# The output product of a gated decoder block as seven products of halves

## The chip, the cores and the metric

The kernel runs on one core of a Trainium2 chip, in one launch. The metric is the device time of an execution in microseconds; each run reports one, and a kernel is judged by the median of its runs. TensorE is written PE, VectorE DVE, ScalarE ACT, GpSimd POOL; PEld is PE's weight load, and SP is the engine that issues most of the DMAs.

## The reference, cut to what matters

A decoder block of 2048 tokens and 1024 channels, in float32. A combined input projection feeds a convolution branch and a dilated attention branch; both are projected, gated and added to y, and y goes through the output product:

```python
y = jax.nn.sigmoid(m_conv) * y_conv + jax.nn.sigmoid(m_attn) * y_attn   # (1, 2048, 1024)
out = y @ w_out                                                         # w_out: (1024, 1024)
x = (x + gate[:, None] * out).astype(dt)                                # gate: (1, 1024)
```

`gate` has one value per output channel, the same for all tokens. It comes from the conditioning vector and is known early in the kernel.

## The kernel before, in words

Each float32 operand of a large product is split into a high part (a copy rounded to the type that PE takes, fp32r) and a low part (the rest), and a product is the sum of three: high by high, high by low, low by high. A product of depth 1024 is therefore 8 x 3 = 24 matmuls of 128x128 by 128x512 for a tile of 128x512.

The kernel's last three stages are these.

- **ya** (attention projection), then **yc** (convolution projection). yc runs over t, four stretches of 512 tokens, and in each over dm, eight blocks of 128 output channels: 24 matmuls, then two DVE operations (the gate `mc` times the sum, plus the stored `ya`), then a store to `y_d` in DRAM. The tiles `yl` (loads of `ya_d`) and `yc` of a block come from one tag, `yt`, of four buffers. Eight banks of PSUM are handed out under four tags of two each; yc's blocks go round three of them (`z`, `s`, `o`).
- **out** (lines 1396 to 1415): over j, 16 blocks of 128 tokens. y is loaded for two blocks at a time into the buffer `wide`, transposed already (channels on partitions); ACT and DVE split it; for each half of 512 output channels 24 matmuls sum into one bank, DVE multiplies by `gate_row` (L1413), adds the residual x (L1414), and the tile is stored.

The engines other than PE get their order from the framework's planner, which lets an instruction go ahead of others of its engine as soon as its inputs and its buffer are there. PE's order is the program's, up to the end of yc before the change. To place side work between PE's matmuls, the kernel keeps a plan: `at_block(n, m, f)` calls f ahead of matmul m of block n (n = 8 t + dm). So the norm of the convolution branch for stretch t is worked out during t - 1 (`norms[t].load`, `.mean`, `.variance` with an rsqrt on POOL, `.spread` with matmuls that need it, `.apply`), and w_out is split during the last stretch:

`split_big(h, l, src)` (L1102 to L1109) loads a tile of 128x512 into a raw buffer, copies it on ACT (high part) and subtracts on DVE (low part). Its raw buffer has the tag `fraw`; in these stages it comes from the pool `ys`, with three buffers:

```python
            raw = big.get("raw", big["fr"]).tile([P, 512], F32, tag="fraw", name="fraw", bufs=3 if "raw" in big else 2)
```

The places for split weights: `wcp` (four pairs of tiles, used by the first half of w_conv_out until dm = 3 of the last stretch), `quarter_tile(kh, t, ...)` (places of the input projection's operands, (0, 2) free after dm = 3 as well, (0, 0) and (1, 0) used by the second half of w_conv_out to the end of yc), `wop` (opened at the start of the last stretch, after the norm's data `lnp` is closed) and `op` (opened there too, on the memory of the norm's scratch and of u for even stretches).

The input projection, earlier in the kernel, is done already as seven products of halves (`quad`, L954: `paab`, `pbab`, `pcab` and their like), with the sums of the weight made on POOL and products that share a bank added up there. Its constant list `PRODUCTS` names the seven pairs.

## Time and profile before

| what | value |
| --- | --- |
| median of 3 runs | 2435.33 us (2433.37 to 2435.88) |
| span of the profiled execution, from first to last instruction | 2433.6 us |
| PE busy | 2395.2 us (98%), 12881 matmuls |
| PEld busy | 2138.5 us (88%) |
| DVE busy | 1688.0 us (69%) |
| ACT busy | 975.0 us (40%) |
| POOL busy | 766.9 us (32%) |
| mean granted TensorE clock | 0.994 |
| DMA moved | 372.99 MB, 153 GB/s on average |

The profiled execution has its span as its time; the three runs are times of other executions and stand within 2.3 us of it. Matmuls overlap their neighbours, so the busy share of PE is no measure of its peak: the distance from one matmul's start to the next is. In grouped rows the columns are the count, the busy time in us with the mean of one in ns, and the idle time of the engine ahead of them with what ended it. In rows by tile they are minimum, median and maximum in ns, then the first and the last start. In rows by stretch they are the length, the busy time and count of PE, PEld, DVE, ACT and POOL, the granted clock, the DMA engines' busy share and GB/s.

### The profile page before, as it was taken

What the parts mean: (1) busy time and instruction counts of PE and PEld (TensorE: products, weight loads), DVE (VectorE), ACT (ScalarE), POOL (GpSimd) and SP (SyncE); (2) the same over time, 40 slices, a digit from 0 to 9 for tenths busy, and PEclk for the clock granted to TensorE, in tenths of its full rate; (3) what the DMA queues carried; (4) which work ended last, traced back from release to release, by engine and by line L of the source; (5) the groups of instructions that cost most, each with busy time, mean ns of one, the idle gap of its engine ahead of it and who ended that gap; (6) DMA issues with size and microseconds to landing.
All of it is one profiled execution on the core that took longest, in us unless ns stands there. A gap on an engine that the chain in (4) does not pass through costs nothing.

```text
span 2433.6 us, 39444 instructions
## 1 busy us (share of the span) xinstructions
PE 2395.2 (98%) x12881; PEld 2138.5 (88%) x12881; DVE 1688.0 (69%) x3891; ACT 975.0 (40%) x2738; POOL 766.9 (32%) x899
## 2 busy tenths in 40 slices
PE   7999999999999999999999999999999999999999
PEld 3989999999999999999888888878888888888887
DVE  5855655555555565557779999989999968864333
ACT  5733333433344344345544444554444444331000
POOL 4421111111111111112467777765655620000000
PEclk8999999999999999999999999999999999999999
DMA  7633543444452222116663544664444479866443
GB/s 260 219 111 109 160 126 100 147 145 144 147 151 85 68 71 58 32 47 197 200 197 129 161 156 160 208 204 128 141 143 143 152 251 321 274 197 214 126 147 100
DMA packets 342219, 372.99 MB, mean 153 GB/s; under 512 B 29752, under 2 KB 243032, under 8 KB 342014
## 3 DMA queue, kind: packets, MB, share of 16 engines
q1 hardware_dynamic: 328718, 346.80, 45.9%
q10 hardware_dynamic: 13296, 23.66, 2.7%
q8 instruction: 103, 1.69, 0.3%
q14 instruction: 102, 0.84, 0.1%
HBM read 231.74 MB, written 138.61 MB: 152 GB/s over the span
## 4 chain that ended last, share of the span: by engine, by line
PE 92%; DVE 1%; ACT 1%; POOL 1%; DMA 1%; issue 0%; SPq 0%; POOLq 0%; DVEq 0%; ACTq 0%
PE pz L369 31%; PE yc L1230 7%; PE out L1230 7%; PE paab L954 7%; PE ya L1230 4%; PE pag_g_d L954 4%; PE pcab L954 4%; PE pag_mc_d L954 4%; PE pag_ma_d L954 3%; PE ps L441 3%; PE po L460 3%; PE pzg L369 3%; PE pbab L954 2%; PE pcg_mc_d L954 2%; PE pcg_g_d L954 2%; PE ptq L431 2%
## 5 line engine op out<-in xcount | busy, mean ns | idle before, releaser
L369 PE MATMUL pz<-wh_u,hT_lo 128*128 128x384 f32 x1536 | 537.6, 350 | 4.4 <-DVE hT_lo L288 2.5
L369 PE MATMUL pz<-wh_u,hT_hi 128*128 128x384 f32 x1536 | 519.5, 338 | 4.5 <-ACT wh_u L345 2.0
L369 PE MATMUL pz<-wl_u,hT_hi 128*128 128x384 f32 x1536 | 520.5, 339 | 0.4 <-DVE wl_u L348 0.4
L397 DVE SCALAR_TENSOR_TENSOR qk<-pz,st,wqk 128x128 f32<-128x128 f32 x384 | 117.0, 347 | 320.5 <-POOL st L113 320.4
L112 POOL TENSOR_SCALAR st<-st 128x2 f32<-128x2 f32 x192 | 47.7, 248 | 813.9 <-ACT sq L386 813.9
L369 PEld LDWEIGHTS pz<-wh_u,hT_hi 128*128 128x128 f32 x1536 | 291.5, 190 | 7.2 <-ACT wh_u L345 2.9
L369 PEld LDWEIGHTS pz<-wh_u,hT_lo 128*128 128x128 f32 x1536 | 290.0, 189 | 7.4 <-DVE hT_lo L288 3.2
L369 PEld LDWEIGHTS pz<-wl_u,hT_hi 128*128 128x128 f32 x1536 | 290.7, 189 | 1.9 <-DVE wl_u L348 1.4
L433 ACT ACTIVATE qkT<-ptq 128x256 f32<-128x256 f32 x192 | 73.9, 385 | 419.9 <-PE ptq L431 419.4
L1032 DVE SCALAR_TENSOR_TENSOR ce<-us,pair_taps,ce 128x512 f32<-128x512 f32 x240 | 180.3, 751 | 1.7
L1003 DVE SCALAR_TENSOR_TENSOR ce<-ut,chan,ce 128x512 f32<-128x512 f32 x240 | 180.1, 751 | 0.0
L1016 DVE SCALAR_TENSOR_TENSOR cq<-ut,chan,cq 128x512 f32<-128x512 f32 x208 | 156.6, 753 | 4.2
L918 POOL TENSOR_TENSOR slT<-wT,shT 128x512 fp32r<-128x512 f32 x97 | 128.7, 1328 | 75.7 <-ACT shT L917 74.6
L386 ACT ACTIVATE sq<-pz 128x128 bf16<-128x128 f32 x384 | 106.2, 276 | 100.3 <-PE pz L369 93.4
L113 POOL TENSOR_TENSOR st<-st,mhalf 128x2 f32<-128x2 f32 x192 | 136.5, 711 | 16.0
L917 ACT ACTIVATE shB<-wB 128x512 fp32r<-128x512 f32 x120 | 75.5, 630 | 150.4 <-issue 44.5
L917 ACT ACTIVATE shT<-wT 128x512 fp32r<-128x512 f32 x100 | 63.1, 631 | 153.1 <-issue 64.6
L918 POOL TENSOR_TENSOR slB<-wB,shB 128x512 fp32r<-128x512 f32 x77 | 102.0, 1324 | 68.0 <-ACT shB L917 66.4
L446 ACT ACTIVATE sm<-sm,osb 128x128 f32<-128x128 f32 (+1 forms) x192 | 88.8, 463 | 62.6 <-DVE osb L444 59.5
L1413 DVE TENSOR_TENSOR ot<-out,gate_row 128x512 f32<-128x512 f32 x32 | 22.1, 692 | 116.2 <-PE out L1230 116.2
L460 PE MATMUL po<-lv,pT 128*128 128x128 f32 x600 | 97.2, 273 | 0.0
L460 PEld LDWEIGHTS po<-lv,pT 128*128 128x128 f32 x600 | 93.0, 189 | 0.5 <-issue 0.5
(624 smaller groups left out, 6288.7 us busy)
## 6 DMA issues: line engine op xcount, KB each, us to landing
wB<-in_w_in_dram SPq DMA_DIRECT2D x140, 256.0 KB, 3.8
qkv_d<-qkv SPq DMA_DIRECT2D x128, 192.0 KB, 2.2
wT<-tT_d SPq DMA_DIRECT2D x80, 256.0 KB, 2.8
raw_u<-in_w_in_dram SPq DMA_DIRECT2D x93, 192.0 KB, 3.3
lqk<-qkv_d SPq DMA_DIRECT2D x128, 128.0 KB, 2.3
tT_d<-wB ACTq DMA_DIRECT2D x60, 256.0 KB, 2.3
acc_d<-osb SPq DMA_DIRECT2D x192, 65.0 KB, 1.6
at<-acc_d SPq DMA_DIRECT2D x64, 195.0 KB, 3.5
```

The source lines that it names most:

```text
L113: nc.gpsimd.tensor_tensor(dst, scratch[:, :n], mhalf[:, :n], op=ALU.pow)
L369: nc.tensor.matmul(pz[:, :width], part(a, k, P * j, P), w[:, :width], start=(m == 0), stop=(m == 23))
L386: nc.scalar.activation(sq, pz[:, P * i : P * i + P], AF.Square, scale=1.0 / math.sqrt(P), accum_out=st[:, i : i + 1])
L397: nc.vector.scalar_tensor_tensor(qk[:, 2 * i : 2 * i + 2].rearrange("p a b -> p (a b)"), pz[:, P * i : P * i + P], st[:, 2 + i : 3 + i], w ...
L460: nc.tensor.matmul(po[:, :P], box["pT"][:, P * i : P * i + P], vt, start=(i == 0), stop=(i == nk - 1))
L917: nc.scalar.activation(h, q[name], AF.Copy)
L918: eng.tensor_tensor(l, q[name], h.bitcast(F32), op=ALU.subtract)
L954: nc.tensor.matmul(ps, w, x, start=(m == 0 and ps.name not in first), stop=(m == 11 and not more), skip_group_check=True)
L1003: stt(box["e"], e[:, 1 + j : 513 + j], chan[:, cb, 2 * j : 2 * j + 1], box["e"], op0=ALU.mult, op1=ALU.add)
L1016: stt(box["o"], o[:, 2 + j : 514 + j], w, psum_o, op0=ALU.mult, op1=ALU.add)
L1032: stt(dst, box["both"][:, 1 + j : 513 + j], pair_taps[:, cb, j : j + 1], box["e"], op0=ALU.mult, op1=ALU.subtract if j == 0 else ALU.add)
L1230: nc.tensor.matmul(pz, w, xx, start=(m == 0), stop=(m == len(terms) - 1))
```

## The change: what it does

The output product is computed by the Winograd form of Strassen's scheme, seven products of halves for eight. Tokens are halved (block j and block j + 8), inner channels are halved (k = 0 to 3 and 4 to 7), and so are output channels. For each of eight pairs of token blocks ("quads") there are seven products of 12 matmuls, 128x128 by 128x512, each into one of three banks; products that belong to the same output tile are added up in the bank, and DVE adds the bank to the residual x in SBUF after each product.

- The sums of y (S1 to S4) are made on POOL, four operations of 128x512 per quad; `y_split(j, n)` then splits the operand of product n on ACT and DVE, five products ahead (`LEAD`).
- The weight is multiplied by `gate` and its sums (T1 to T4) are made during yc. `gate_rows` loads the gate twice 128x512; `wo_fetch(k)` loads 1 MB of w_out into the buffer `wide`; `wo_sums(k)` runs six POOL operations on it, with T3, T2 and T4 in buffers of the tag `fraw` of `ys`, and stores all seven 128x512 tiles to `wo_d` in DRAM. There are four k, fetched at blocks 11, 14, 17, 20 and summed at 12, 15, 18, 21.
- `wo_split(name, k)` splits a tile of `wo_d` with `split_big`: 20 during the last stretch of yc (B11, B21, T2, then T1 and T3), eight during the first quad (B22, T4), whose places yc holds to its end.
- y is loaded by `y_load(j)` in four tiles (`wide` for the first quad, freed buffers of u after), x by `x_load(j)`; the multiplication of the result by the gate is gone, and so is `gate_row` (L1413).
- PE's order is now the program's to the end.

The diff, cut to its core:

```diff
+    wo_d = dram.tile([7, 4, P, 512], F32, name="wo_d")
...
-    def split_wo(half, k):
-        h, l = (last["wo"][half].tile([P, 512], F32R, name=f"wo{half}{hl}{k}", bufs=1) for hl in "hl")
-        split_big(h, l, w_out[P * k : P * k + P, 512 * half : 512 * half + 512])
-        last[half, k] = h, l
+    WO_SLOT = {"B11": 0, "T1": 1, "B21": 2, "B22": 3, "T3": 4, "T2": 5, "T4": 6}
+    WO_ORDER = [b for _, b in PRODUCTS]
...
+    def wo_fetch(k):
+        w = wo_raw[k] = sp.tile([P, S], F32, tag="wide", name=f"wo_raw{k}").rearrange("p (h c n) -> p h c n", h=2, c=2)
+        nc.sync.dma_start(w, w_out.rearrange("(h k p) (c n) -> k p h c n", h=2, p=P, c=2)[k])
+
+    def wo_sums(k):
+        w = wo_raw.pop(k)
+        for c in range(2):
+            nc.gpsimd.tensor_tensor(w[:, :, c], w[:, :, c], last["gate"][c][:, None, :].to_broadcast([P, 2, 512]), op=ALU.mult)
+        t3, t2, t4 = (ys.tile([P, 512], F32, tag="fraw", name=f"wo{n}_{k}", bufs=3) for n in ("T3", "T2", "T4"))
+        for dst, x0, x1 in ((t3, w[:, 1, 1], w[:, 0, 1]), (w[:, 0, 1], w[:, 0, 1], w[:, 0, 0]),
+                            (t2, w[:, 1, 1], w[:, 0, 1]), (t4, w[:, 1, 0], t2)):
+            nc.gpsimd.tensor_tensor(dst, x0, x1, op=ALU.subtract)
+        nc.sync.dma_start(wo_d[:4, k].rearrange("q p n -> p q n"), w.rearrange("p h c n -> p (h c) n"))
+        for n, t in (("T3", t3), ("T2", t2), ("T4", t4)):
+            nc.sync.dma_start(wo_d[WO_SLOT[n], k], t)
...
+    at_block(8, 6, gate_rows)
+    for k in range(4):
+        at_block(11 + 3 * k, 6, lambda k=k: wo_fetch(k))
+        at_block(12 + 3 * k, 6, lambda k=k: wo_sums(k))
...
-            for k in range(KC):
-                at_block(KC * t + k, 5, lambda k=k: split_wo(0, k))
-                at_block(KC * t + k, 15, lambda k=k: split_wo(1, k))
+            for i, (name, k) in enumerate((b, k) for b in WO_ORDER[:3] for k in range(4)):
+                at_block(KC * t + i // 3, 3 + 7 * (i % 3), lambda name=name, k=k: wo_split(name, k))
+            for i, (name, k) in enumerate((b, k) for b in WO_ORDER[3:5] for k in range(4)):
+                at_block(KC * t + 4 + i // 2, 3 + 10 * (i % 2), lambda name=name, k=k: wo_split(name, k, (nc.vector, nc.gpsimd)[k % 2]))
...
+    def y_split(j, n):
+        a11, a12, a21, a22 = ysrc[j]
+        pool_tt = nc.gpsimd.tensor_tensor
+        if n == 0:
+            s1 = ysrc[j, "S1"] = ys.tile([P, 512], F32, tag="fraw", name=f"ys1_{j}", bufs=3).rearrange("p (k t) -> p k t", k=4)
+            pool_tt(s1, a21, a22, op=ALU.add)
+            pool_tt(a21, a11, a21, op=ALU.subtract)
+        if n == 2:
+            pool_tt(a11, ysrc[j, "S1"], a11, op=ALU.subtract)
+            pool_tt(a12, a12, a11, op=ALU.subtract)
+        src = (a11, a12, a11, ysrc[j, "S1"], a21, a12, a22)[n]
+        h, l = ya_of[j, n] = [op.tile([P, 4, P], F32R, tag=f"y{hl}", name=f"y{hl}{j}_{n}") for hl in "hl"]
+        nc.scalar.activation(h, src, AF.Copy)
+        nc.vector.tensor_tensor(l, src, h.bitcast(F32), op=ALU.subtract)
+
+    def out_quad(j, hooks):
+        pa, pb, pc = bank("z", f"oa{j}"), bank("s", f"ob{j}"), bank("o", f"oc{j}")
+        x11, x12, x21, x22 = xin.pop(j)
+        add = lambda dst, ps: nc.vector.tensor_tensor(dst, dst, ps, op=ALU.add)
...
+        product(0, pa, True)
+        add(x11, pa)
+        product(1, pb)
+        add(x11, pb)
+        store(0, x11)
+        product(2, pa, True)
+        add(x12, pa)
+        product(3, pc, True)
+        add(x22, pc)
+        product(4, pa, True)
+        add(x22, pa)
+        store(3, x22)
+        product(5, pc)
+        add(x12, pc)
+        store(1, x12)
+        product(6, pa)
+        add(x21, pa)
+        store(2, x21)
...
+            if j == 0 and n < 2:
+                for k in (2 * n, 2 * n + 1):
+                    wo_split(WO_ORDER[5], k, (nc.vector, nc.gpsimd)[k % 2])
+            elif j == 0 and n < 6:
+                wo_split(WO_ORDER[6], n - 2, nc.vector)
+            at = 7 * j + n + LEAD
+            if at < 7 * HB:
+                y_split(at // 7, at % 7)
...
     pe_order.__exit__(None, None, None)
-            po = bank("zo"[half], f"out{half}_{j}")
-            project(po, [yh[:, k] for k in range(KC)], [yl[:, k] for k in range(KC)],
-                    [last[half, k][0] for k in range(KC)], [last[half, k][1] for k in range(KC)])
-            nc.vector.tensor_tensor(ot, po, gate_row[:, cols], op=ALU.mult)
-            nc.vector.tensor_add(ot, ot, xt)
```

More of the change, by code (lines that the diff above doesn't have):

```diff
@@ new lines, in wo_place @@
+    def wo_place(name):
+        if name in ("B11", "B21"):
+            return [last["wo"][0].tile([P, 4, 512], F32R, name=f"wo{hl}{name}") for hl in "hl"]
+        if name == "T2":
+            return [last["wo"][1].tile([P, 4, 512], F32R, name=f"wo{hl}{name}", bufs=1) for hl in "hl"]
+        if name == "T3":
+            rows = [[wcp.tile([P, 512], F32R, tag=f"w{hl}{k}", name=f"wo{hl}{name}{k}") for k in range(4)] for hl in "hl"]
+            return rows
+        return [quarter_tile(*{"T1": (0, 2), "B22": (0, 0), "T4": (1, 0)}[name], hl, f"wo{hl}{name}") for hl in ("hi", "lo")]
@@ new lines, in tile_hybrid_block, with y_load @@
+    ysrc, ya_of, xin = {}, {}, {}
+    HB = NB // 2
+    def y_load(j):
+        if j == 0:
+            tiles = sp.tile([P, S], F32, tag="wide", name="yq0").rearrange("p (q k t) -> p q k t", q=4, t=P)
+            tiles = [tiles[:, q] for q in range(4)]
+        else:
+            tiles = [up[1].tile([P, 4, P], F32, tag="ul", name=f"yq{j}_{q}", bufs=KC) for q in range(4)]
+        ysrc[j] = tiles
+        for q in range(4):
+            jj, kh = j + HB * (q // 2), q % 2
+            nc.sync.dma_start(tiles[q], y_d[4 * kh : 4 * kh + 4, :, P * jj : P * jj + P].rearrange("k p t -> p k t"))
@@ new lines, in tile_hybrid_block, with out_hooks, f @@
+    LEAD = 5
+    y_load(0)
+    x_load(0)
+    for n in range(LEAD):
+        y_split(0, n)
+    def out_hooks(j):
+        def f(n):
+            if j == 0 and n < 2:
[6 more added lines that the diff above has]
+                y_split(at // 7, at % 7)
+        return f
@@ L1416, in tile_hybrid_block @@
+    for j in range(HB):
+        if j + 1 < HB:
+            y_load(j + 1)
+            x_load(j + 1)
+        out_quad(j, out_hooks(j))
+    pe_order.__exit__(None, None, None)
     op_c.__exit__(None, None, None)
```

54 lines of the change are left out of this document (33 added, 21 removed).

## The prediction

> **What bounds the kernel now.** I read the chain of work that ended last first, for the stretch that the change touches, then the grouped instructions and the timeline of that stretch, and last the queues around it.
>
> ```profile
> span 2433.6 us, 39444 instructions
> ...
> 2158.82 92.78 PE yc L1230 x396
> 2251.59 177.48 PE out L1230 x768
> 2429.07 0.02 issue
> 2429.09 0.70 DVE ot L1413
> 2429.82 0.69 DVE ot L1414
> ```
>
> From 2158.82 to 2429.07 nothing but matmuls is on the chain, and the output product alone holds 177.48 us in 768 of them, 231 ns each. It begins where the convolution product (yc) ends, without a gap. So a matmul that is left out is worth its full pace, as long as every other engine and queue still arrives in time. The other engines of that stretch have room:
>
> ```profile
> L1414 DVE TENSOR_TENSOR ot<-ot,xt 128x512 f32<-128x512 f32 x32 | 22.2, 692 | 1.1
> L1413 DVE TENSOR_TENSOR ot<-out,gate_row 128x512 f32<-128x512 f32 x32 | 22.1, 692 | 116.2 <-PE out L1230 116.2
> ...
> L1108 ACT ACTIVATE wo1h<-fraw 128x512 fp32r<-128x512 f32 x8 | 5.0, 631 | 27.4 <-PE yc L1230 18.3 <-DMA fraw<-in_w_out_dram 9.2
> ```
>
> DVE waited 116.2 us for the output product's matmuls. The third row is the warning of this case: the splits of the output weight waited 18.3 us for yc to free their place, and 9.2 us for their data.
>
> **The products.** Before: 16 token blocks x 2 halves x 24 matmuls = 768. After: 8 quads x 7 products x 12 = 672 of the same 128x128 by 128x512 shape. Their pace depends on where the moving weight lies:
>
> ```profile
> 2262.50 0.40 PE L1230 MATMUL out<-wo0h,yh 128*128 128x512 f32 x1
> ...
> 2268.11 0.40 PE L1230 MATMUL out<-wo1h,yh 128*128 128x512 f32 x1
> ...
> 2273.59 0.40 PE L1230 MATMUL out<-wo0h,yh 128*128 128x512 f32 x1
> ```
>
> These are the first matmuls of three runs of 24: with the weight in the pool wop, (2268.11 - 2262.50)/24 = 233.8 ns; in the pool op, where y lies too, (2273.59 - 2268.11)/24 = 228.3 ns. After the change one product of seven (T2) has its weight in op. For the six in other places (wop, wcp, the quarter tiles) I take 233.8, as the nearest row; the lower bound is the input projection's quads, which also run seven products of 12:
>
> ```profile
> 1226.58 2.72 PE pbab L954 x12
> 1229.30 2.72 PE paab L954 x12
> ```
>
> That is 226.7 ns. The sum: 96 x (6 x 233.8 + 228.3) ns = 156.6 us, so 177.5 - 156.6 = **20.9 us less**; at 226.7 throughout it is 152.3 us and 25.1 less. The two rows above also show one product following another without a gap while two products share a bank, which is the structure that the change copies.
>
> **The drains.** The multiplication by the gate (L1413) goes, and each product is added to the residual straight from its bank. Per quad DVE has 7 additions and 7 splits of 0.69 us, 9.7 us; ACT 7 copies of 0.63, 4.4 us; both beside 19.6 us of matmuls. A bank is taken up again one product later at the earliest, so an addition of 0.69 us has 2.8 us of cover; if DVE were later than that, PE would wait. I cost it at nothing. At the very end one DVE operation stands in place of two: **0.7 us less**. The issues on SP stay at 12 per quad (four y, four x, four out) against nine per two blocks, over 19.6 us, and hide behind the matmuls too.
>
> **The weight's new path.** This is where I expect the gain to shrink. Before, splits read w_out from DRAM. Now wo_fetch and wo_sums run four turns through the one buffer "wide": load 1 MB, six POOL operations (two of 1024 columns, four of 512), store 1 MB and three tiles T3, T2, T4; only then may the next turn load, and after the fourth y_load(0) uses the same buffer.
>
> ```profile
> L1400 SPq DMA_DIRECT2D yw<-y_d x8: 370/374/385, 2123.3 to 2387.5; - x8
> ...
> L918 POOL TENSOR_TENSOR slB<-wB,shB 128x512 fp32r<-128x512 f32 x77 | 102.0, 1324 | 68.0 <-ACT shB L917 66.4 <-DMA wT<-tT_d 1.4
> L1109 POOL TENSOR_TENSOR wal<-wa,wah 128x512 fp32r<-128x512 f32 x4 | 6.0, 1528 | 5.3 <-ACT wah L1108 5.3
> ...
> d<-u_d SPq DMA_DIRECT2D x4, 512.0 KB, 10.1
> ...
> y_d<-yc SPq DMA_DIRECT2D x32, 256.0 KB, 4.0
> ...
> fraw<-in_w_out_dram SPq DMA_DIRECT2D x16, 256.0 KB, 5.8
> ```
>
> The buffer comes free at 2123.3, where the first yw load is issued today. A POOL turn is worth 8 x 1.32 = 10.6 us by the first POOL row and 8 x 1.53 = 12.2 by the second; I take 11, nearer the row with more counts. For a load of 1 MB I take 6 us and for the larger store 7: 256 KB land after 4.0, 512 KB after 10.1 where four of them ran together. A turn is 24 us, and the fourth sum ends at 2123.3 + 6 + 3 x 24 + 11 = 2212.3.
>
> Until then no split can start, although the first parts lie in DRAM long before. A pool hands out its buffers in program order:
>
> ```profile
> L1345 SPq DMA_DIRECT2D ya_d<-yt x32: 319/320/1271, 1975.3 to 2071.5; - x32
> ...
> L1384 SPq DMA_DIRECT2D yl<-ya_d x32: 319/424/837, 2068.6 to 2242.2; - x32
> ```
>
> The yl tiles share four buffers with yt; their data was stored from 1975.3 on, yet the first yl load was issued at 2068.6, beside the last yt stores. In the same way the T tiles of all four sums stand ahead of the splits' raws in the three buffers "fraw". Behind them queue, in this order: 20 splits (B11, B21, T2, T1, T3), the sum S1 of the first y quad, four of B22, one of T4, S1 of the second quad, three of T4. How fast they pass:
>
> ```profile
> 2207.96 0.33 SPq L1107 DMA_DIRECT2D fraw<-in_w_out_dram  x1
> ...
> 2227.31 0.33 SPq L1107 DMA_DIRECT2D fraw<-in_w_out_dram  x1
> ...
> L1109 DVE TENSOR_TENSOR wo1l<-fraw,wo1h x8: 684/692/694, 2207.2 to 2232.4; 128x512 fp32r<-128x512 f32 x8
> ```
>
> These are the first and the last of ten loads and the last split that they feed, which ends at 2232.4 + 0.7 = 2233.1. Ten loads through three buffers are four turns of the first one, so a turn takes 25.1/4 = 6.3 us.
>
> The last split that the first quad needs, T4 of k = 3, stands at place 29 of that queue. Counted from the end of the fourth sum: 4.0 us until its T4 tile is stored and gives up its buffer, six split turns of 6.3 (37.8), S1 of quad 0 (three POOL operations read or write with it, 4.5), a B22 split (6.3), S1 of quad 1 (4.5), T4 itself (6.3): 63.4 us, or 2212.3 + 63.4 = 2275.7. PE would want it after six products and nine matmuls from 2251.6, 2251.6 + 18.8 = 2270.4. So the first quad waits **5.3 us** in all, part of it already before product 2, which needs S2 = S1 - A11. Bounds: nothing, if the transfers land 1 us or more faster each; 35 us by the upper rows (below). From quad 1 on nothing of this is left.
>
> What else the new path is moved past: wo_fetch and the T stores stand in SP's queue ahead of mc, yl and y_d transfers, so a late store holds those up; yc's blocks have six banks of 5.6 us each before PE notices, so up to about 28 us of lateness there costs nothing. On POOL the sums share the queue with the rsqrt of the last norm, which is a rival below.
>
> **The sum.** The profiled span of 2433.6 us lies at the lower end of the three runs (2433.37 to 2435.88); I carry the difference to their median, 1.7 us, through. 2435.3 - 20.9 - 0.7 + 5.3 = **2419.0 us**, 0.67% less. A measurement of this kernel tells about 0.2%, 4.9 us, from no change.
>
> A wait of PE can cost more than itself.
>
> ```profile
> 1160.00:1164.00 4.00, 1.08 (x9) 0.88 (x8) 3.60 (x10) 3.04 (x10) 2.25 (x3) 0.97 0.61 184
> ```
>
> In this stretch PE was busy for 1.08 us of 4, and the granted clock fell to 0.97, just behind the gap. The Trainium skill (TensorE: Matmul & The Clock Gate, Part 1) says that an idle window of some 3.4 us drops the clock to half until a busy window has passed; by that rule a first quad that waits in one piece would pay an estimated 1.7 us more, 2420.7 in place of 2419.0; the row agrees that the clock falls, and does not show for how long.
>
> **The rivals.**
> No wait at all: the fourth sum ends before 2207. For it speaks that the transfers run into a queue that is busy only in part between 2149 and 2201:
>
> ```profile
> 2149.00:2175.00 26.00, 26.00 (x121) 21.28 (x120) 16.94 (x28) 8.62 (x13) 1.25 (x2) 1.00 0.58 174
> 2175.00:2201.00 26.00, 26.00 (x112) 20.90 (x112) 12.15 (x19) 4.21 (x7) 0.00 (x0) 1.00 0.56 181
> ```
>
> (DMA share 0.58 and 0.56.) With 5 us each way the sum ends at 2123.3 + 5 + 3 x 21 + 11 = 2202.3: 2435.3 - 21.6 = 2413.7. Chance 0.23.
>
> The rsqrt of the last norm stands behind the second sum on POOL, if that was queued first.
>
> ```profile
> 2151.41 0.79 PE pc L1266 x8
> 2152.20 5.72 PE yc L1230 x24
> 2157.93 0.89 PE pr L1275 x8
> ...
> L113 POOL TENSOR_TENSOR stf<-stf,mhalf 128x4 f32<-128x4 f32 x4 | 4.1, 1032 | 0.3
> L112 POOL TENSOR_SCALAR stf<-stf 128x4 f32<-128x4 f32 x4 | 1.3, 322 | 179.6 <-DVE stf L1268 179.6
> ```
>
> PE gives the variance at 2152.2 and wants the result at 2157.9. The second load lands at 2153.3; a sum and the rsqrt after it (0.32 + 1.03 us) end near 2153.3 + 11 + 1.4 = 2165.7, so PE waits 7.8 us in the middle of yc. The queue of the splits goes on meanwhile, so the 5.3 us later are hidden: 2435.3 - 21.6 + 7.8 = 2421.5. Against it: the variance is ahead in the program. Chance 0.08.
>
> POOL turns slower than its rows. Each of its six operations would wait for one DVE operation of 0.69 us: 12.2 + 4.1 = 16.3 us per turn. The fourth sum ends at 2123.3 + 6 + 3 x 29.3 + 16.3 = 2233.5, the first quad waits 26.5 us, and the time is 2440.2, no longer faster. The two POOL rows differ by 0.2 us and give it little weight so far, but DVE mostly read PSUM beside the first of them. Chance 0.08. The Trainium skill (SBUF — State Buffer, "SBUF: two separate sides") has this as a lock that a two-input DVE operation and a reading GpSimd operation take in turn, the other blocked for the whole of it; by that rule 2440.2, by the rows alone 2419.0.
>
> Slower: the one buffer "wide" as the bound. By the upper rows (10.1 us each way, 12.2 on POOL) a turn takes 32.4 us, the fourth sum ends at 2123.3 + 10.1 + 97.2 + 12.2 = 2242.8, and the first quad waits 35.8 us: 2449.5. It decides from 21.6 us of waiting, a fourth sum that ends at 2228.6, turns of 29.4 us. For it speaks that 11 MB are added to the queue between 2123 and 2220, against it the half empty queue shown above. Chance 0.13.
>
> The product does not run dense: additions queue on DVE behind splits that wait for POOL's S tiles. With 0.5 us at each of 32 returns to a bank, 16 us go on top of the forecast: 2435.0. The input projection's quads speak against it. Chance 0.09.
>
> **How the numbers follow.** The forecast's case, waits of 2 to 16 us in the first quad, has 0.39. The predicted time is its 2419.0. Faster: 0.39 + 0.23 + 0.08 = 0.70, less 0.03 for a forecast that comes out near the next bound: 0.67. Within 0.2%: the dense product's failure and most of the case of slow POOL turns, 0.15. Slower: the rest, 0.18. The range begins below the case without waits, part of the way to the faster pace (2413.7 - 4.2 would be all of it), at 2411.5, and reaches to 2438.0, which leaves out the slow chain and half of the case of slow POOL turns.
>
> **What would show it.** Right: 672 matmuls of about 233 ns under L1230's successor, six POOL operations per sum with the fourth ending near 2212, the first quad some 25 us long and the other seven 19.6 each, DVE additions of 0.69 us without PE behind them. Waits of PE on ACT or DVE for B22 or T4 in the first quad are the expected loss. Wrong: quads after the first that are longer than 20 us, or a first quad with nothing to wait for (then 2413.7), or one that waits over 21.6 us.

## The result and the profile after

The changed kernel takes 2446.35 us, median of five runs (2444.05 to 2448.34); the kernel before took 2435.88 us beside it (2433.37 to 2440.42, five runs). The ratio is 1.0040, with a 95% interval of 1.0027 to 1.0052: slower by 0.4%, where 0.7% less had been forecast. The profiled execution took 2444.05 us.

The chain of work that ended last, in order of time (start, length):

```profile
span 2442.1 us, 39625 instructions
...
2149.28 8.71 DMA wo_raw<-in_w_out_dram
...
2166.23 2.08 PE pr L1276 x8
2168.31 94.18 PE yc L1231 x396
2262.49 2.81 PE oa L1486 x12
2265.30 2.81 PE ob L1486 x12
...
2275.70 5.33 DMA fraw<-wo_d
...
2281.81 5.47 PE oa L1486 x12
...
2306.90 2.76 PE oa L1486 x12
...
2438.35 0.69 DVE xt L1474
```

Before, yc began its last long run at 2158.82 and the output product at 2251.59; now these are 2168.31 and 2262.49. The output stage takes 2438.35 - 2262.49 = 175.9 us in place of 177.5. Its matmuls are as short as hoped: a product takes 2.76 to 2.81 us, and from the second quad on the quads follow each other without a gap, 19.58 us each. So the 20.9 us are there, and PE loses them again. Its waits from 2060 on (us in total, times, longest):

```profile
PE oa L1486 <- ACT wohiB L1109: 13.7, 1, 13.7
PE pr L1276 <- POOL stf L114: 7.7, 1, 7.7
PE oc L1486 <- DVE xt L1474: 2.5, 1, 2.5
```

The table by stretch around the long wait shows what it costs besides (length, busy time and count of PE, PEld, DVE, ACT and POOL, granted clock, DMA share, GB/s):

```profile
2268.00:2282.00 14.00, 0.29 (x2) 0.22 (x2) 10.51 (x15) 5.83 (x12) 3.13 (x3) 0.58 1.00 318
2282.00:2286.00 4.00, 4.00 (x10) 3.13 (x11) 2.16 (x2) 0.45 (x1) 3.92 (x4) 0.50 1.13 338
2286.00:2290.00 4.00, 4.00 (x16) 3.17 (x15) 2.50 (x4) 1.68 (x3) 1.98 (x2) 0.83 1.06 390
```

After the wait the granted clock is 0.50, and the third product takes 5.47 us in place of 2.80. The first quad is 16.2 us of waits and 3.0 us of slow matmuls too long, 19.2. After the rsqrt it is the same: the eight matmuls `pr` take 2.08 us (before 0.89) and the run behind them 94.18 (before 92.78), 2.6 us. The difference of the spans is then: yc starts 0.7 later, `pr` comes another 7.6 later, 2.6 are lost behind it, the output stage is 1.6 shorter and the tail 0.7, which makes +8.6; it is 2442.1 - 2433.6 = 8.5.

Why the rsqrt came late, on POOL's timeline:

```profile
2158.12 5.09 POOL L1375 TENSOR_TENSOR wo_raw<-wo_raw,gate 128x1024 f32<-128x1024 f32 x2 [13.10 <-DMA wo_raw<-in_w_out_dram]
2163.30 0.55 POOL L113 TENSOR_SCALAR stf<-stf 128x4 f32<-128x4 f32 x1
2163.93 1.26 POOL L1379 TENSOR_TENSOR woT<-wo_raw 128x512 f32<-128x512 f32 x1
2165.15 1.02 POOL L114 TENSOR_TENSOR stf<-stf,mhalf 128x4 f32<-128x4 f32 x1
```

POOL stood idle for 13.1 us until the second load of w_out landed, in front of the two multiplies by the gate. The norm's two small operations (L113, L114) stood behind these, and one subtraction between them.

The sums also slow DVE. During the first sum POOL and DVE take turns, one operation each every 1.70 us:

```profile
2138.29 1.62 POOL L1379 TENSOR_TENSOR woT<-wo_raw 128x512 f32<-128x512 f32 x1
2140.00 1.62 POOL L1379 TENSOR_TENSOR wo_raw<-wo_raw 128x512 f32<-128x512 f32 x1
```
```profile
2138.69 1.78 DVE L1293 TENSOR_TENSOR u_5l<-vf,u_5h 128x512 fp32r<-128x512 f32 x1
2140.39 1.78 DVE L1286 SCALAR_TENSOR_TENSOR vf<-d,chan,rs 128x512 f32<-128x512 f32 x1
```

Before, with POOL idle, the first of these DVE operations (then L1292) took:

```profile
2134.19 0.69 DVE L1292 TENSOR_TENSOR u_5l<-vf,u_5h 128x512 fp32r<-128x512 f32 x1
```

Over the whole of yc the addition `yc<-yc,yl` takes 989 ns on average in place of 690. What this costs in time was not tried by itself.

What ended the first quad's wait, on the timelines of DVE and SP:

```profile
2280.37 0.69 DVE L1110 TENSOR_TENSOR woloB<-fraw,wohiB 128x512 fp32r<-128x512 f32 x1 [3.31 <-ACT wohiB L1109]
2280.98 0.68 DVE L1474 TENSOR_TENSOR xt<-xt,oa 128x512 f32<-128x512 f32 x1
```
```profile
2273.74 0.92 SPq L1453 DMA_DIRECT2D xt<-in_x_dram  x2
2275.19 0.42 SPq L1453 DMA_DIRECT2D xt<-in_x_dram  x1
2275.70 0.86 SPq L1108 DMA_DIRECT2D fraw<-wo_d  x2
```

The third product uses the bank of the first, so it needs the addition at 2280.98, which ends at 2281.66. (The profile puts the wait down to ACT's copy `wohiB` because that one ended last, at 2281.70; but it belongs to B22, which only the sixth product uses.) The addition stood on DVE behind a split of B22, whose quarter had just been loaded; and its own x tile had been asked for at 2275.19 only, with 5.8 us from issue to landing in this stretch (`--tile xt`). The order of SP's queue, taken from the program, says why:

```
xt1_0, xt1_1, all yq1 (second quad), y_d<-yc3_6, xt1_2, xt1_3, raw, xt0_0 (first quad), raw, raw, yq2_0 (third quad),
y_d<-yc3_7, xt0_1, xt0_2, rest of yq2, all xt2 (third quad), first output store, raw of T4, xt0_3, ...
```

x for the first quad goes to the buffers `yt`, which yc's last drains hold, and the planner puts the loads of the second quad (2 MB) ahead of it. The last quarters of T4 stand behind the third quad's loads as well. In the profiled execution yc's last store was issued at 2277.13 (before: 2253.07), and these loads went out as much later.

### The profile page after: what moved, and what is told of

Read it like the earlier page. It is cut to its first block, busy times and chain, and to the rows that moved or that the text cites. A ratio compares the mean times of both kernels' runs of the same rounds, so it can differ in the third digit from the quotient of the medians.

```text
span 2442.1 us, 39625 instructions
## 1 busy us (share of the span) xinstructions
PE 2378.3 (97%) x12785; PEld 2124.1 (87%) x12785; DVE 1730.6 (71%) x3929; ACT 998.8 (41%) x2790; POOL 859.7 (35%) x961
## 4 chain that ended last, share of the span: by engine, by line
PE 88%; DMA 5%; DVE 3%; ACT 1%; POOL 1%; issue 1%; SPq 1%; ACTq 0%; DVEq 0%; POOLq 0%
PE pz L370 32%; PE paab L955 7%; PE yc L1231 6%; PE ya L1231 4%; PE oa L1486 4%; PE pcab L955 4%; PE pag_mc_d L955 4%; PE pag_g_d L955 3%; PE pag_ma_d L955 3%; PE ps L442 3%; PE po L461 3%; PE pzg L370 2%; PE pbab L955 2%; PE pcg_mc_d L955 2%; PE ptq L432 2%; PE oc L1486 2%
## 5 line engine op out<-in xcount | busy, mean ns | idle before, releaser
L113 POOL TENSOR_SCALAR st<-st 128x2 f32<-128x2 f32 x192 | 47.3, 246 | 812.8 <-ACT sq L387 812.8
L114 POOL TENSOR_TENSOR st<-st,mhalf 128x2 f32<-128x2 f32 x192 | 136.6, 711 | 16.0
L445 DVE CUSTOM_DVE_ANT_0 sm<-ps,mask 128x128 f32<-128x128 f32 (+1 forms) x192 | 68.5, 357 | 26.5 <-PE ps L442 26.5
```

The lines of the kernel that those rows point to most:

```text
L114: nc.gpsimd.tensor_tensor(dst, scratch[:, :n], mhalf[:, :n], op=ALU.pow)
```

## The experiments

Every run stands against the kernel before, on the same chip; the ratio carries the comparison (0.1% is 2.4 us), and where two runs are compared by their medians the text says so. The kernels with "plain" in their name leave the gate and the sums out of the weight, so their output is another one. The last two columns are read from the trace. "Starts" is the first matmul of the output product. "Over" is how much longer the first quad is than a dense one: from that matmul to the second product of the second quad, less eight products of 2.80 us.

| kernel | median us | ratio [95%] | starts | over, us |
| --- | --- | --- | --- | --- |
| changed kernel | 2446.35 | 1.0040 [1.0027, 1.0052] | 2262.3 | 19.2 |
| rsqrt_first | 2444.39 | 1.0032 [1.0021, 1.0044] | 2253.3 | 25.5 |
| op_raws | 2440.71 | 1.0017 [1.0008, 1.0027] | 2262.4 | 15.2 |
| op_raws_rsqrt | 2441.69 | 1.0018 [1.0008, 1.0028] | 2250.8 | 25.8 |
| plain | 2425.49 | 0.9955 [0.9938, 0.9972] | 2251.6 | 11.4 |
| x0_own | 2442.28 | 1.0021 [1.0010, 1.0031] | 2264.9 | 17.7 |
| x0_hold | 2439.24 | 1.0011 [1.0001, 1.0020] | 2264.6 | 13.0 |
| x0_hold_rsqrt | 2436.71 | 0.9997 [0.9988, 1.0006] | 2254.0 | 20.7 |
| x0_hold_plain | 2419.44 | 0.9936 [0.9919, 0.9952] | 2251.0 | 5.9 |
| all4 | 2435.97 | 0.9994 [0.9985, 1.0003] | 2254.2 | 15.4 |
| all4_kmajor | 2436.95 | 1.0003 [0.9994, 1.0012] | 2255.6 | 14.4 |
| kmajor_early | 2434.30 | 0.9995 [0.9986, 1.0004] | 2251.9 | 13.5 |
| kmajor_poolq | 2433.52 | 0.9986 [0.9977, 0.9996] | 2255.7 | 10.0 |
| gate_drain_only | 2433.46 | 0.9984 [0.9975, 0.9993] | 2255.5 | 12.0 |
| gate_drain_rsqrt | 2423.49 | 0.9950 [0.9934, 0.9967] | 2252.7 | 6.4 |
| gate_drain_b2 | 2425.68 | 0.9960 [0.9946, 0.9974] | 2254.8 | 5.8 |
| gate_drain_pool | 2422.99 | 0.9949 [0.9932, 0.9965] | 2252.8 | 7.1 |
| gate_drain_raw5 | 2426.99 | 0.9960 [0.9946, 0.9974] | 2256.2 | 7.5 |
| x0_hold_plain_traffic | 2421.97 | 0.9942 [0.9928, 0.9957] | 2254.6 | 6.9 |

### One wait, two waits, or the weight's path

The theories at the start. A: the queue of splits (three raw buffers, fed by four turns of `wide`) sets the end of the first quad, whatever PE does before. B: the rsqrt and the first quad are two losses that add up. C: the added traffic fills the DMA engines. D: the quads lose by themselves.

**rsqrt_first** queues the second sum behind the last norm's rsqrt on POOL.

```diff
     def wo_sums(k):
+        if k == 1:
+            with tc.issue_after(norms[3].rsqrt.ins):
+                return wo_sum_ops(k)
...
-        at_block(12 + 3 * k, 6, lambda k=k: wo_sums(k))
+        at_block((12, 16, 18, 21)[k], 6, lambda k=k: wo_sums(k))
```

> One edit to the changed kernel: the second weight sum is queued on POOL behind the last norm's rsqrt. Theory A (the splits' queue of three raw buffers, fed by four turns of the one buffer, sets the end of the first quad, whatever PE does before): the wait of 7.7 us in the convolution product and its 2.6 us at half clock go, the first quad's waits grow by about 10 us from 19.2, the time stays at 2446 (2443 to 2449). Theory B (two independent losses): the first quad's waits stay near 19, the time falls to 2436.

The waits of PE from 2060 on in rsqrt_first:

```profile
PE oa L1492 <- DVE xt L1480: 18.9, 1, 18.9
PE oc L1492 <- DVE xt L1480: 2.7, 1, 2.7
```

The wait for the rsqrt is gone, the output product starts 9.0 us sooner, and the first quad gives 6.3 of them back (A wanted about 10). This is nearer to A than to B: the first quad waits for something that comes at its own time.

**plain** splits the quarters straight from w_out.

```diff
-        split_big(h, l, wo_d[WO_SLOT[name], k], eng)
+        split_big(h, l, w_out[512 * kh + P * k : 512 * kh + P * k + P, 512 * c : 512 * c + 512], eng)
...
-        at_block(11 + 3 * k, 6, lambda k=k: wo_fetch(k))
-        at_block(12 + 3 * k, 6, lambda k=k: wo_sums(k))
```

> The changed kernel with the weight's new path left out: no gate, no sums of the weight (the 28 splits read the quarters of the output weight itself, so the output is another). Theory A: no wait of PE on the weight, eight quads of 19.6 us, 2414 us. Theory D (the quads lose by themselves, additions late on DVE or the y and x transfers): quads longer than 20 us or a first quad that still waits, more than 2420. If only the traffic of the path mattered, it is 2414 too; the next run tells these apart.

Its waits, and its chain at the first quad:

```profile
PE oa L1483 <- DVE xt L1471: 4.9, 1, 4.9
PE oc L1483 <- DVE xt L1471: 3.1, 1, 3.1
```
```profile
2250.57 5.02 DMA yq<-y_d
2255.60 5.70 DMA xt<-in_x_dram
...
2262.23 4.43 PE oa L1483 x12
```

Against the changed kernel 20.9 us are gone by the medians. But 2414 was expected, and 11.4 us of the first quad remain with no sum in the program. The chain names them: the x tile of the first quad, asked for at 2255.60 behind the second quad's y. That is theory E below.

**op_raws** gives the 28 quarters six raw buffers of their own; **op_raws_rsqrt** adds the order of rsqrt_first.

```diff
-        split_big(h, l, wo_d[WO_SLOT[name], k], eng)
+        split_big(h, l, wo_d[WO_SLOT[name], k], eng, raw=op.tile([P, 512], F32, tag="wraw", name=f"wraw{name}{k}", bufs=6))
-            op_c = pool("op", bufs=9)
+            op_c = pool("op", bufs=7)
```

> The changed kernel with six raw buffers of their own for the 28 splits, in the pool op, paid for by two of the nine y buffers; transfers and POOL work are the same. Theory A: the splits no longer queue behind the T tiles and pass faster, the first quad's waits fall from 19.2 to under 5 us, the wait on the rsqrt stays: 2427 to 2431. Theory C (DMA is saturated by the added traffic): the waits stay, 2440 to 2447.

> Both edits: own raw buffers, and the second sum behind the rsqrt. Theory A: no wait in the convolution product, under 8 us in the first quad (it begins 10 us earlier than with own buffers alone), 2415 to 2422. Theory B: 2417. Theory C: 2433 to 2440.

5.6 us for the buffers alone by the ratios, and nothing more with the rsqrt in order: a start 11.6 us sooner turned into 10.6 us more of waiting. A's 2427 to 2431 and 2415 to 2422 are both missed: the three shared buffers are part of the loss, not its cause. The numbers lie nearer to C's (the second is 1.7 us above its band), which is taken up below.

### The order of SP's queue

Theory E: the first quad's x and the last quarters stand on SP behind some 4 MB of loads that the second and third quads need later. **x0_own** gives the first quad's x four buffers in `op`; **x0_hold** also queues the second quad's x and all of the third quad's loads behind T4's last quarter; **x0_hold_rsqrt** adds the order on POOL, **x0_hold_plain** the loads of plain.

```diff
-        own, tag, n = (ys, "yt", 4) if j == 0 else (up[1], "uh", KC)
-            t = own.tile([P, 512], F32, tag=tag, name=f"xt{j}_{q}", bufs=n)
+            t = op.tile([P, 512], F32, tag=f"x0{q}", name=f"xt0_{q}", bufs=1) if j == 0 else up[1].tile([P, 512], F32, tag="uh", name=f"xt{j}_{q}", bufs=KC)
...
-    y_load(0)
     x_load(0)
+    y_load(0)
...
+        if j == 0:
+            y_load(1)
+        elif j == 1:
+            with tc.issue_after(last["raw"].ins):
+                x_load(1)
+                y_load(2)
+                x_load(2)
```

> The four x tiles of the first quad get buffers of their own (8 KB, taken from the y pairs, nine down to eight) and are loaded before the last token tile's drains, in place of waiting for the drains' own buffers. Theory E (SyncE's queue: the first quad's x and the last raw quarters stand behind about 4 MB of loads for the second and third quads): the x tile is no longer late, but the raw quarters of B22 and T4 still stand behind the prefetch, so the first quad loses 10 to 19 us instead of 19: 2438 to 2446. Theory A (the four turns of the wide buffer set when B22 and T4 are split): 2444 to 2447.

> As x0_own, and the x loads of the second quad and all loads of the third are queued on SyncE behind T4's last raw quarter. Theory E: B22 and T4 are split in time, only the wait for the last norm's rsqrt (7.7 us and its slow start 2.6) and a few us at the first quad are left: 2428 to 2436. Theory A: as in the changed kernel, 2442 to 2447, since the raw quarters come no sooner than the sums and the three raw buffers let them.

> As x0_hold, and the second sum stands behind the last norm's rsqrt on GpSimd. Theory E: 2418 to 2430. Theory A: the sums end later, so the first quad waits longer than before the hold: 2440 to 2446.

> As x0_hold, with the raw quarters straight from w_out: the gate and the sums are left out of the weight, so the output differs. Theory E (in the kernel without the sums the 11 us that are left against 2414 are the order of SyncE's queue): 2413 to 2417. Rival C (the traffic itself: the quads' loads, x and the raw quarters together fill the DMA engines at the start of the out stage): 2421 to 2426.

With the sums in place E is worth 7 us by the ratios (1.0040 to 1.0011), the rsqrt on top of it 3.4 us more: 0.9997, no longer slower. x0_own came out as E expected; x0_hold lies between E and A, and x0_hold_rsqrt over 6 us above E. Without the sums it takes 6 us off plain by the medians (4.6 by the ratios), 2419.4, 2 us over the forecast of E. So the order is one cause and not the main one. What still waits in x0_hold_plain is one wait of 4.1 us:

```profile
PE oa L1483 <- DVE xt L1471: 4.1, 1, 4.1
```

### Volume, position, or the gate

Theory F: 28 quarters twice through memory, after sums that end too late, are too much for the 45 us that are left. **all4** puts together what was found: x0_hold_rsqrt, and four raw buffers of their own. **all4_kmajor** splits B11, B21 and T2 in the order of k, so that nine of these twelve quarters need only the first three sums.

```diff
-    wo_d = dram.tile([7, 4, P, 512], F32, name="wo_d")
+    wo_d = [dram.tile([7, P, 512], F32, name=f"wo_d{k}") for k in range(4)]
...
-            for i, (name, k) in enumerate((b, k) for b in WO_ORDER[:3] for k in range(4)):
+            for i, (name, k) in enumerate((b, k) for k in range(4) for b in WO_ORDER[:3]):
```

> The sums and the gate stay in the weight as in the changed kernel; four raw buffers of their own for the 28 quarters (the y pairs go from nine to six), own x buffers for the first quad, the prefetch of the later quads held behind T4's last raw quarter, the second sum behind the last norm's rsqrt. Theory A+E (raw buffers shared with the sums, and SyncE's order): all waits but a few us are gone: 2418 to 2428. Theory F (the sums end some 6 us too late and 28 quarters of 256 KB through memory twice are too much for the 45 us that are left, whatever the buffers): 2432 to 2438, as x0_hold_rsqrt.

> As all4, with a memory tensor of its own for each quarter row of the weight, and the splits of the first three parts in the order of the rows, so that nine of twelve need only the first three sums. Theory A+E: no more than 3 us faster than all4. Theory F: 3 to 8 us faster than all4, since nine splits no longer stand behind the fourth sum.

all4 stays at 2436.0, in F's band. all4_kmajor misses F's forecast: it is no faster. The load of its first quarter was issued at 2223.09 only, behind the stores of the fourth sum on SP. **kmajor_early** moves these stores behind the nine loads, and the three quarters that need the fourth sum behind those of T1 and T3; **kmajor_poolq** leaves the order of all4_kmajor and has POOL issue the stores and the last three loads of `wide`, so that SP waits for no sum.

```diff
+        if k == 3:
+            with tc.issue_after(last["raw"].ins):
+                return wo_sum_ops(k)
```
```diff
-        nc.sync.dma_start(wo_d[k][WO_SLOT[n]], t)
+        nc.gpsimd.dma_start(wo_d[k][WO_SLOT[n]], t)
```

> As all4_kmajor, and the stores of the fourth sum stand on SyncE behind the nine loads that need only the first three sums (in all4_kmajor they stood ahead of them, and the first quarter was loaded at 2223). Theory Q (it is the position: twenty quarters have to be loaded after the fourth sum): the first quarter is loaded by 2205, the first quad's wait falls from 10 to under 4 us, 2424 to 2430. Theory V (it is the volume: the DMA engines are as full before the fourth sum as after it): 2432 to 2437.

> all4_kmajor with the stores of the sums and the last three loads of the wide buffer issued by GpSimd's own queue in place of SyncE's, so that nothing on SyncE waits for the sums; the bytes are the same. Theory Q (SyncE's queue stands still behind the stores of the sums, and with it the last token tile's loads and stores and the quarters): the first quarter is loaded by 2205, the first quad waits under 5 us, 2422 to 2429. If the sums themselves come too late whatever the queue: 2433 to 2438.

kmajor_early lands in V's band. But neither brought the first quarter under 2205, as theory Q had wanted (2214.05 and 2211.30), so Q was tried only in part. kmajor_poolq is the best with the gate in the weight, 0.14% under before, 4 us or more short of Q's band and within the band for sums that come too late whatever the queue. Its fourth sum ends later than ever, at 2229.3. The volume by itself was tried with **x0_hold_plain_traffic**, which adds 14 copies of 256 KB that nothing waits for:

```diff
+            if t == NT - 1 and dm < 7:
+                with tc.issue_after(landed.ins):
+                    for h in range(2):
+                        nc.sync.dma_start(wo_d[dm // 2, 2 * (dm % 2) + h], w_out[P * dm : P * dm + P, 512 * h : 512 * h + 512])
```

> x0_hold_plain (no gate, no sums, so the output differs) with 14 copies of 256 KB from memory to memory put beside the last token tile's work, two behind each gate load, that nothing waits for: about the 3.6 MB by which the changed kernel moves more than x0_hold_plain from 2213 to 2262. Theory V (the volume fills the DMA engines and delays the loads that the first quad needs): the first quad waits 8 us or more instead of 4.1, 2425 to 2434. Theory Q (it is not the volume but the loads that can only start behind the fourth sum): 2418 to 2422.

The traffic from 2213 to 2262, in x0_hold_plain, in x0_hold_plain_traffic, and in the changed kernel:

```profile
DMA packets 7729, 10.62 MB, mean 217 GB/s; under 512 B 646, under 2 KB 3206, under 8 KB 7725
```
```profile
DMA packets 9458, 13.76 MB, mean 281 GB/s; under 512 B 841, under 2 KB 3401, under 8 KB 9454
```
```profile
DMA packets 9266, 14.21 MB, mean 290 GB/s; under 512 B 814, under 2 KB 2862, under 8 KB 9261
```

With 3.1 MB more in this stretch the time grows by 2.5 us by the medians and 1.5 by the ratios, whose intervals overlap. In the profiled executions the output product starts 3.6 us later and the first quad grows by 1.0; PE waits 5.0 us there where V wanted 8, and the time lies in Q's band. Nearly the changed kernel's volume is thus not what makes 19 us there. (The traffic of the sums before 2213 is not in this test.)

**gate_drain_only** puts the gate of the changed kernel back to the drain, two DVE operations a product. The weight keeps only the four subtractions, and B11, B21 and B22 are split from w_out itself.

```diff
-        for c in range(2):
-            nc.gpsimd.tensor_tensor(w[:, :, c], w[:, :, c], last["gate"][c][:, None, :].to_broadcast([P, 2, 512]), op=ALU.mult)
...
-        nc.sync.dma_start(wo_d[:4, k].rearrange("q p n -> p q n"), w.rearrange("p h c n -> p (h c) n"))
-        for n, t in (("T3", t3), ("T2", t2), ("T4", t4)):
+        for n, t in (("T1", w[:, 0, 1]), ("T3", t3), ("T2", t2), ("T4", t4)):
...
+        if name[0] == "B":
+            kh, c = int(name[1]) - 1, int(name[2]) - 1
+            src = w_out[512 * kh + P * k : 512 * kh + P * k + P, 512 * c : 512 * c + 512]
...
-        add = lambda dst, ps: nc.vector.tensor_tensor(dst, dst, ps, op=ALU.add)
+        def add(dst, ps):
+            g = op.tile([P, 512], F32, tag="gx", name=f"gx{j}", bufs=2)
+            nc.vector.tensor_tensor(g, ps, last["gate"][int(dst is x12 or dst is x22)], op=ALU.mult)
+            nc.vector.tensor_tensor(dst, dst, g, op=ALU.add)
```

> The changed kernel with this one thing changed: the gate goes back to the output's drains, so B11, B21 and B22 come straight from w_out and the sums have four subtractions; x buffers, order of loads and of rsqrt as in the changed kernel (the y pairs go from nine to eight for the drain's buffers). If the gate in the weight is what turns the change into a loss: 2426 to 2433. If the loads' order is needed for it as well: 2434 to 2442.

From 1.0040 to 0.9984 (half a us above the first band): the gate's place alone is worth 0.56%, 13.6 us, and turns the loss into a small gain. In the profiled execution the output product starts 6.8 us sooner (no wait for the rsqrt is left) and the first quad is 7.2 us shorter. The move brings three things at once, which no run takes apart: eight multiplies leave POOL, 12 of 28 stored tiles (3 MB) fall away, and the 12 quarters of B11, B21 and B22 need no sum. **gate_drain_rsqrt** adds x0_hold_rsqrt to it, and **gate_drain_b2** two more raw buffers, for the quarters that come from w_out.

> The gate goes back to the output (each product's drain multiplies by the gate, then adds: 8 DVE operations more a quad); the weight path keeps the four subtractions alone, and B11, B21, B22 come straight from w_out, so 8 multiplies on GpSimd and 12 of 28 stores are gone; own x buffers, the hold and the order of rsqrt as before; raw buffers still the three that the sums use. Theory F and A both: 2418 to 2428. Theory D (the quads cannot take more on DVE: 16 us of 19.6 a quad): quads longer than 20.5 us, 2428 to 2436.

> As gate_drain_rsqrt, with two raw buffers of their own for the quarters that come straight from w_out, so that B11 and B21 wait for no sum. If the ring of three shared raw buffers still sets the first quad: 2 to 6 us faster than gate_drain_rsqrt (2415 to 2424); if not, the same within 1.5 us.

gate_drain_rsqrt takes 2423.49 us, 0.50% under the kernel before and 0.9% under the changed one. Its sums (tile `wo_raw`: minimum, median, maximum in ns, first and last start) beside those of the changed kernel:

```profile
L1384 POOL TENSOR_TENSOR woT<-wo_raw,woT x4: 1621/1626/1749, 2136.4 to 2190.0; 128x512 f32<-128x512 f32 x4
```
```profile
L1375 POOL TENSOR_TENSOR wo_raw<-wo_raw,gate x8: 2343/2819/3517, 2131.9 to 2209.7; 128x1024 f32<-128x1024 f32 x8
L1379 POOL TENSOR_TENSOR woT<-wo_raw,woT x4: 1278/1453/1626, 2143.4 to 2217.4; 128x512 f32<-128x512 f32 x4
```

The last operation of the fourth sum starts at 2190.0 in place of 2217.4, 27 us sooner, and the first quarter is loaded at 2190.85 (2217.72). On the chain the quads after the first stay dense, although DVE has seven operations more in each (15.0 us busy from 2284.42 to 2304.00; 10.6 in a quad of the changed kernel), so for them D is out:

```profile
2263.09 4.52 PE oa L1497 x12
...
2284.42 2.76 PE oa L1497 x12
...
2304.00 2.76 PE oa L1497 x12
```

(2304.00 - 2284.42 = 19.58.) gate_drain_b2 is not faster, so the ring of three is not what is left, unless the pair of y buffers that it gives up (six for seven) costs what its own buffers win. **gate_drain_pool** moves the low parts of B22 and T4 to POOL, and **gate_drain_raw5** gives these eight quarters two buffers of their own.

```diff
-                    wo_split(WO_ORDER[5], k, (nc.vector, nc.gpsimd)[k % 2])
+                    wo_split(WO_ORDER[5], k, nc.gpsimd)
...
-                wo_split(WO_ORDER[6], n - 2, nc.vector)
+                wo_split(WO_ORDER[6], n - 2, nc.gpsimd)
```

> As gate_drain_rsqrt, with the eight low parts of B22 and T4 subtracted on GpSimd, so that the first quad's first drain stands behind no split on VectorE. If that queue makes the last 4.6 us wait: 2416 to 2420. If the drain waits for something else: 2422 to 2426.

> gate_drain_pool with two raw buffers of their own for the eight quarters of B22 and T4 (the y pairs go from seven to six), so that these loads don't wait for the ring of three. If the ring sets the last 4 us of waiting at the first quad and the slow start behind it: 2416 to 2420. If the loads wait for something else: 2421 to 2426.

gate_drain_pool is as fast as gate_drain_rsqrt (2422.99, 0.9949), so DVE's queue is not what is left either; of all versions with the gate and the sums in them these two are the fastest. gate_drain_raw5, which also has a y pair fewer, is 4 us slower than gate_drain_pool by the medians, 2.7 by the ratios, whose intervals overlap; at 2426.99 it misses both bands. Its chain shows the quarter of B22 asked for at 2261.82, on SP behind the second quad's y, which waits for yc's buffers:

```profile
2261.82 4.25 DMA wrawB<-in_w_out_dram
...
2266.09 0.63 ACT wohiB L1109
...
2272.21 5.26 PE oa L1500 x12
```

So here a free buffer was worth nothing behind a queue that stands. That this order makes the last 4 us in the other versions too was not tried.

## Why the prediction was wrong, point by point

- **The products**: right. 156.6 us was forecast for eight quads; the dense quads of 19.58 us make 8 x 19.58 = 156.6.
- **The tail**: right, 0.69 us after the last matmul in place of 1.4.
- **The drains**: right from the second quad on. In the first quad the addition waited on DVE behind a split, and for an x tile that wasn't there. The prediction gave that tile's load no buffer and no place in SP's queue; it counted the issues per quad and not what stands ahead of the first.
- **The four turns of `wide`**: nearly right. Turns of 24 us were forecast; the sums began at 2131.89, 2158.12, 2182.21 and 2207.30, 25.1 us apart on average, and the fourth ended at 2218.6, not 2212.3. The reasoning that every quarter stands behind the fourth sum held: the first was loaded at 2217.72.
- **The first quad's wait, 5.3 us: the step that failed.** With PE on time (rsqrt_first) the first quad is 25.5 us too long. The last split of T4 was to end at 2275.7; in the changed kernel it ends at 2298.3 (DVE `woloT`, two from 2295.96 on, 2.38 us). The sums account for 6.3 us of that (2218.6 in place of 2212.3), the queue behind them for 16.3: 79.7 us in place of 63.4. Two parts of the loss are shown. The gate's way through the weight is the largest: 13.6 us of the time by the ratios (gate_drain_only). The order on SP and the x buffers are worth some 5 to 7 us, with the sums or without (x0_hold, x0_hold_plain). About 6 us stay in the first quad in the best versions, and their cause is open. The working took the turn of a raw buffer, 6.3 us, from the kernel before, where ten quarters passed and no sum, and followed the buffers alone. It did not count that SP runs through one list in order: quarters, yc's loads and stores, and the next quads' prefetch hold each other up.
- **Lateness of SP "up to about 28 us costs nothing"**: right for yc's banks, PE never waited for a drain of yc there. But yc's last store went out 24 us later than before (2277.13 against 2253.07), and the buffers `yt` that x of the first quad needs come free with it. The cost lay behind yc.
- **The rsqrt**, given 0.08, happened: 7.7 us against 7.8 forecast, with the place and the reason named. That the size agrees so closely is luck: the second load landed at 2158.0 and not at 2153.3, 4.7 us later, and the rsqrt stood behind three of the sum's six operations and not behind all, which saved about as much. Nor was its second half wrong: the splits' queue goes on meanwhile, and so taking that wait away wins only 2 us by the medians. But with a first quad 25 us late instead of 5, that no longer meant that nothing was lost. The slow start after it (2.6 us) was in no sum.
- **The slow clock**: the forecast carried 1.7 us as an estimate from the Trainium skill (TensorE: Matmul & The Clock Gate, Part 1) beside its sum. The trace agrees that the clock falls to half (0.50 from 2282 to 2286), and shows a larger loss: 2.7 us behind the 13.7 us of waiting and 2.6 behind the 7.7, for half the clock lasted some 5.6 us (0.50 from 2281.81 to 2287.40). Behind 4.6 us it was 1.7 (4.52 - 2.80 in gate_drain_rsqrt). Shorter waits differ: 1.8 behind 3.1 us (4.58 - 2.80 in plain), 0.2 behind 2.5 us (3.04 - 2.80). The row of before that the prediction shows is the stretch in which PE waited; the stretch behind it, 1164 to 1170, has a granted clock of 0.74, and six us at 0.74 are about 1.6 us lost.
- **POOL slower by the shared port**: hardly. A subtraction of 512 columns took 1.26 us with DVE idle and 1.63 beside it, and a sum 11.3 to 13.1 us where 16.3 were feared. But DVE paid: 1.78 us in place of 0.69. The Trainium skill (SBUF — State Buffer, "SBUF: two separate sides") has the lock as one that blocks whichever of the two comes second. The trace agrees that they take turns (1.70 us for a pair), though a pair takes less than 1.26 + 0.69 = 1.95. The rival charged all of it to POOL.
- **The slow chain of `wide`** (2449.5) has the number nearest to the result and not its mechanism: it wanted turns of 29.4 us or more.

In the prediction's own terms: 2435.3 - 20.9 - 0.7, both as measured, + 19.2 for the first quad + 10.2 for the rsqrt and its slow start + 0.7 of a later yc is 2443.8; the profiled execution took 2444.05. (The 1.7 us that the sum carries from the span to the median are the way in which times are taken: in all runs the reported time is 1.7 to 2.3 us above the span of the same execution, 2444.05 and 2442.1 here. The span is not the execution's time, as the part ahead of the prediction has it.)

What stays open: with the gate in the weight, own buffers, the order on SP and an own queue for the sums still left the first quad 10 to 15 us too long (all4 to kmajor_poolq), and no single one of them settled it. Shown is that with the gate at the drain most of it is gone, and that volume alone in the last 50 us does not make it. That the sums, which then end 27 us sooner, are the reason fits the traces and is not shown apart from the fewer stores and from the 12 quarters that wait for no sum.

## What to carry to other kernels

A factor that can be multiplied in at the drain is not free when it moves into the weight: then every part of the weight has to pass the stage that multiplies, and here the first split waited for the last sum. A drain with two DVE operations a product, hidden under 2.8 us of matmuls from the second quad on, beat it by 13.6 us. Before costing new loads at nothing, write down one queue in its order, with each entry's buffer and the event that frees it: the loads that the first tile needs stood behind up to 4 MB for later tiles. And a wait that ends when another chain ends is not shortened by reaching it sooner; what counts is the time at which that chain ends.

## What the runs showed of the hardware that was not expected

- A product takes 5.47 us in place of 2.80 after PE waited 13.7 us, and 4.4 to 5.5 after waits of 3.8 to 4.9 us (gate_drain_pool, x0_hold_plain, gate_drain_rsqrt, plain): each such wait costs 1.6 to 2.7 us more than itself. Below that the length alone does not decide: 4.58 after 3.1 us (plain) and after 2.75 us (x0_hold_plain_traffic), but 3.04 after 2.5 us.
- A POOL subtraction of 128x512 takes 1.26 to 1.29 us where DVE has little to do (2163.93 and 2215.99 in the changed kernel) and 1.62 beside a busy DVE, 0.4 more. The DVE operation beside it takes 1.78 us in place of 0.69, 1.1 more.
- A store and a load of 1 MB in one transfer took 7.47 us (from 2141.79) and 8.71 us (from 2149.28, above) while the DMA engines' busy share was 0.94 and 1.00.
- 3.1 MB of extra copies, which raised the DMA share from 2213 to 2262 from 0.67 to 0.87, cost 2.5 us by the medians, 1.5 by the ratios.
